# Grouping small matmuls in a planned instruction order, and one vector product for two half tiles

## The chip, the cores and the metric

The kernel runs on one core of one Trainium2 chip, as one program in one launch. The metric is device time in microseconds, from plain runs without the profiler; a further run was made with the hardware profiler, and its rows are quoted. An engine is named as in the profile: PE is TensorE (matmuls; PEld is its weight load), DVE is VectorE, ACT is ScalarE, POOL is GpSimd, SP is the queue that issues DMAs.

## The reference

One layer of a diffusion backbone: 1024 latent tokens and 256 context tokens, width 1024, float32. In order: a modulated SwiGLU feed-forward half step, token mixing, a second feed-forward half step, a final norm. The change lies in token mixing:

```python
def gla_chunked(q, k, v, g, s0):               # 4 heads, dk 64, dv 128, both directions
    b = cumsum(gc, axis=-2)
    rel = exp(where(tri, b_i - b_j, -inf))     # a decay per key feature
    scores = einsum('id,jd,ijd->ij', qc, kc, rel)
    o = scores @ vc + (qc * exp(b)) @ s
    s = exp(b_last) * s + (kc * exp(b_last - b)).T @ vc

def retention_chunked(q, k, v, s0, log_gamma): # 4 heads, dk 128, dv 128, both directions
    scores = (qc @ kc.T) * decay
    o = scores @ vc + (qc * q_dec) @ s
    s = chunk_dec * s + (kc * k_dec).T @ vc
```

Both run forward and backward; latent scans start from the final states of the context scans. The inputs of both are column blocks of one projection `h @ w_in`, and the outputs are normalised, gated with silu of another block and projected with `w_out`.

## The kernel before

**Projections and small products.** A projection multiplies a float32 value split into a high and a low float32r part: three products (high by high, low by high, high by low; `mm3`, lines 401 to 404) of 128x512, 128x288 or 128x256 into a `psa` bank of PSUM. A weight half is loaded to `raw`, ScalarE rounds it to `whi`, VectorE subtracts to `wlo` (`split`, 396 to 398). Everything else on TensorE in mixing works in float32 and writes `psb` banks: transposes against the identity, the products of the scans, and the level products. A float32 matmul shows as two records of TensorE, a transpose as one. There are four `psa` and four `psb` banks.

**The gated scan in levels** (`gla_mix`, 1555 on). For a head and a half of the latent tokens (`tg` 0 and 1) the tile A holds queries of the forward direction on partitions 0 to 63 and keys of the backward one on 64 to 127, B the other two. For half sizes hs of 1, 2, 4, 8, 16, 32, 64, blocks of 2 hs tokens are scored across their middle. Up to hs 16, four copies (two on VectorE, two on ScalarE) bring the halves into zeroed tiles zq and zk, and sixteen matmuls with 32 columns (32 records) make the level's scores in a `psb` bank, which VectorE merges into `cm` or `sc` by a mask. For 32 and 64 the matmuls read A and B directly, in 64x32 and 64x64 pieces. At the end of each level A's upper halves and B's lower halves are multiplied by the decays of the level (lines 1608 to 1611), two VectorE products:

```python
bc = lambda i: e[:, :, i:i + 1].to_broadcast([P, 256 // hs, hs])
nc.vector.tensor_tensor(out=blk(a)[:, :, hi], in0=blk(a)[:, :, hi], in1=bc(0), op=ALU.mult)
nc.vector.tensor_tensor(out=blk(bb)[:, :, lo], in0=blk(bb)[:, :, lo], in1=bc(1), op=ALU.mult)
```

**The gate columns.** `proj_v` (1334) projects the values of two heads, and the first pair's projection carries 32 gate columns: for each of four chunks of 128 tokens the values are copied from `psa` to `vt`, the gate columns to a tile `p89` of two buffers, and that is transposed at once. `ctx_gla` and `ctx_ret` compute the context states of each head; `ctx_ret` scales its values by decays with four `tensor_scalar` products on VectorE before its two 128x256 matmuls.

**What sets the order.** From the second half step's end to the last mixing head, operations aren't issued as they are called: `Recorder` (168 on) keeps them with their reads and writes, and `run` (290 on) makes a list schedule. Each operation has a planned cost (`COST` and `add`, 204 on; VectorE, ScalarE and GpSimd costs times `GROW`, 1.05). `run` repeatedly takes, over all engines, the engine whose next operation can start first, and on it, among those that are ready at that time, the one called earliest. An operation is ready when its predecessors have ended in the plan (plus 0.4 us where TensorE waits for another engine) and its buffers are free. The order found is fixed on each engine, including SP's queue of DMAs; the engines work through their lists in order, and real waits are semaphores. The instructions of this stage all show as line 142 in the profile, so they are told apart by tile. The output projection behind it (`mixed_out`) isn't recorded; its first products come between the last transposes.

Of the kernel before, what the change touches and what calls it, by code (L numbers as in the profile page):

```python
# [11 lines left out]
F32 = mybir.dt.float32  # L12
F32R = mybir.dt.float32r
AF = mybir.ActivationFunctionType
ALU = mybir.AluOpType
PSUM = bass.MemoryType.PSUM

P = 128
# [29 lines left out]
class View:  # L48
# [64 lines left out]
    def bitcast(self, dtype):  # L113
        return self.step(lambda t: t.bitcast(dtype), self.dims)

    def get(self):
        t = self.root.real
        for f in self.how:
            t = f(t)
        return t  # L120
# [40 lines left out]
class Recorder:  # L161
# [42 lines left out]
    def add(self, eng, call, outs, ins, name, a, k):  # L204
        n = lambda v: int(np.prod(v.shape[1:]))
        size = max([n(v) for v in outs] + ([n(v) for v in ins] if name in ("tensor_reduce", "bn_stats") else []) + [1])
        bytes, func = 0, None
        if eng == "PE":
            if name == "transpose":
                cost = 0.11 * size / P  # L210
            elif (a[2].root if isinstance(a[2], View) else a[2]).dtype == F32R:
                cost = (size + 32) / 2400
            else:
                cost = size / 600 + 0.01 if size > 64 else size * 0.0011
        elif eng == "SP":
            v = (outs or ins)[0]
            cost, bytes = 0.42, 4 * size * v.shape[0]
        else:
            base, each = COST.get((eng, name)) or COST[eng]
            cost = 1.2 if k.get("op") == ALU.pow else base + size * each if size > 32 else 0.19  # L220
            if name == "activation":
                func = (a[2] if len(a) > 2 else k["func"])
        op = Op(eng, call, cost, outs, ins, name, bytes, FSET.get(func))
        op.port = eng == "POOL" or name in SHARED and not any(self.psum(v.root) for v in ins)
        (self.ops if self.group is None else self.group).append(op)

# [66 lines left out]
    def run(self):  # L293
        self.link()
        self.rank()
        self.last = {}
        free = {"PE": 0.0, "DVE": LEAD, "ACT": LEAD, "POOL": LEAD, "SP": LEAD}
        port = {"DVE": LEAD, "POOL": LEAD}
        cand, table, pipe, order = [o for o in self.ops if not o.left], None, LEAD, []
        while cand:  # L300
            best = None
            byeng = defaultdict(list)
            for o in cand:
                if o.eng is None:
                    best = (-1e9, o)
                    break
                t = self.room(o)
                if t is not None:
                    for p in o.pre:
                        t = max(t, p.end + (0 if p.eng == o.eng else LATPE if p.eng == "PE" else TOPE if o.eng == "PE" else LATE))  # L310
                    byeng[o.eng].append((t, o.key, o))
            if best is None:
                for eng, os in byeng.items():
                    if eng in port:
                        other = port["DVE" if eng == "POOL" else "POOL"]
                        os = [(max(t, other) if o.port else t, i, o) for t, i, o in os]
                    s = max(free[eng], min(t for t, _, _ in os))
                    o = min((i + (TSW if eng == "ACT" and o.func and o.func != table else 0), i, o) for t, i, o in os if t <= s + 1e-6)[2]
                    if best is None or s < best[0]:
                        best = (s, o)  # L320
            s, o = best
            cand.remove(o)
            if o.eng is None:
                o.end = max((p.end for p in o.pre), default=-1e9)
            else:
                c = o.cost * (1 if o.eng in ("PE", "SP") else GROW)
                if o.eng == "ACT" and o.func and o.func != table:
                    table, c = o.func, c + 1.3
                o.end = s + c
                free[o.eng] = o.end - OVER.get(o.eng, 0)  # L330
                if o.port:
                    port[o.eng] = free[o.eng]
                if o.eng == "SP":
                    pipe = max(pipe, s) + o.bytes / 300e3
                    o.end = max(pipe, s) + DLAT
# [24 lines left out]
        assert len(order) == len(self.ops)  # L360
        t = self.trunk
        t.nc, t.tc = self.nc, self.tc
        del t.tile
        for n, v in self.kept.items():
            setattr(t, n, v)
        return order


class Trunk:
# [964 lines left out]
    def proj_v(self, pr, gla, vt, pool):  # L1334
        nc = self.nc
        for tg in LATTG:
            ps = [self.psA() for _ in range(4)]
            gate = self.v_proj(tg, pr, gla, ps)
            if gate:
                pT = self.psB()  # L1340
            for c in range(4):
                nc.scalar.copy(vt[:, 4 * tg + c, :], ps[c][:, :256])
                if gate:
                    r = self.tile(pool, [P, P], F32, "p89", 2)
                    nc.scalar.copy(r.rearrange("p (k r) -> p k r", k=4), ps[c][:, 256:288].unsqueeze(1).to_broadcast([P, 4, 32]))
                    nc.tensor.transpose(pT[:, c * P:(c + 1) * P], r, self.ident)
            if gate:
                self.p89T[tg] = self.tile(pool, [P, 512], F32R, f"p89T{tg}", 1)
                self.stack(self.p89T[tg], pT, (64, 96))

# [204 lines left out]
    def gla_mix(self, h, vt, qp, kp, sg, gt, pool):  # L1555
        nc = self.nc
        u = h % 2
        f, b = slice(0, 64), slice(64, 128)
        c3 = lambda t: t.rearrange("p (c t) -> p c t", t=P)
        c32 = lambda t: t.rearrange("p (c t) -> p c t", t=32)  # L1560
        A, B, g, L, sc, big, cm = {}, {}, {}, {}, {}, {}, {}
        us = slice(64 * u, 64 * u + 64)
        for tg in LATTG:
            A[tg], B[tg] = self.tile(pool, [P, 512], F32, f"A{tg}"), self.tile(pool, [P, 512], F32, f"B{tg}")
            for t, sl, src in ((A, f, qp), (A, b, kp), (B, f, kp), (B, b, qp)):
                nc.sync.dma_start(t[tg][sl], src[tg][us])
            g[tg], L[tg] = gt[tg]
        for hs in (1, 2, 4, 8, 16, 32, 64):
            blk = lambda t: t.rearrange("p (n t) -> p n t", t=2 * hs)
            lo, hi = slice(0, hs), slice(hs, 2 * hs)  # L1570
            for tg in LATTG:
                a, bb = A[tg], B[tg]
                if hs <= 16:
# [23 lines left out]
                else:  # L1597
                    for o in range(0, 512, 2 * hs):
                        r = o % P
                        l, m, e = slice(o, o + hs), slice(o + hs, o + 2 * hs), o + 2 * hs  # L1600
                        nc.tensor.matmul(big[tg][r:r + hs, m], bb[f, l], a[f, m], start=True, stop=True)
                        nc.tensor.matmul(big[tg][r + hs:r + 2 * hs, l], a[b, m], bb[b, l], start=True, stop=True)
                if hs == 1:
                    e = g[tg]
                else:
                    o = 512 - 1024 // hs
                    e = L[tg][:, o:o + 512 // hs]
                e = e.rearrange("p (n t) -> p n t", t=2)
                bc = lambda i: e[:, :, i:i + 1].to_broadcast([P, 256 // hs, hs])
                nc.vector.tensor_tensor(out=blk(a)[:, :, hi], in0=blk(a)[:, :, hi], in1=bc(0), op=ALU.mult)  # L1610
                nc.vector.tensor_tensor(out=blk(bb)[:, :, lo], in0=blk(bb)[:, :, lo], in1=bc(1), op=ALU.mult)
                if hs == 8:
                    sc[tg] = g[tg]
                    nc.scalar.copy(sc[tg].rearrange("p (c r t) -> p c r t", c=4, r=4),
# [23 lines left out]
        for i in range(7):  # L1638
            for sl, c, d in ((f, i, i + 1), (b, 7 - i, 6 - i)):
                nc.vector.scalar_tensor_tensor(out=S[sl, d, :], in0=S[sl, c, :], scalar=eT(sl, c),  # L1640
                                               in1=U(sl, c), op0=ALU.mult, op1=ALU.add)
        for tg in LATTG:
            po = self.psB()
            with self.pe_order():
                for c in range(4):
                    s = slice(c * P, (c + 1) * P)
# [443 lines left out]


NT2 = 5
AB = 5
AHEAD = 5
NLOW = 150
# [118 lines left out]
```

## Time and profile before

| | us |
|---|---|
| plain runs, median of 3 | 2107.12 (2106.99 to 2107.57) |
| profiled execution | 2112.04 |
| its span, first to last instruction | 2110.2 |
| mean granted TensorE clock | 0.996 |

The page gives each engine's busy time over the span; the stage view gives it between two times, with the clock granted to TensorE (1.00 is full speed). Matmul durations in the rows are longer than the spacing of their starts, since matmuls are pipelined: what one costs is read from the starts. In rows of instructions in order of time the columns are start, duration, engine, line, operation, output and inputs, size and count; a bracket behind it is idle time of the engine before it and what ended it. In rows of groups there stand busy time, mean ns of one, and idle time ahead with its releasers.

### The profile page before, as it was taken

The numbers are of one execution on the slowest core, as the hardware profiler recorded it, in microseconds if no ns is written. First come the engines' busy times: TensorE is split into PE (matmuls) and PEld (weight loads), VectorE is DVE, ScalarE is ACT, GpSimd is POOL, SyncE is SP. The second block draws the span as 40 slices with busy tenths as digits, with TensorE's granted clock in tenths as the row PEclk, the third lists the DMA queues.
The fourth block names the chain that finished last, engine by engine and source line by source line (L and its number), as shares of the span: only waits on it lengthen the run. The fifth ranks groups of instructions, "written<-read, shape, count | busy, mean of one in ns | idle before, by whom it ended". The sixth has DMA issues, their size and how long they took to land. (4 is left out here: it accounts for less than half of the span.)

```text
span 2110.2 us, 34588 instructions
## 1 busy us (share of the span) xinstructions
PE 2082.0 (99%) x12490; PEld 1779.4 (84%) x12490; DVE 1492.1 (71%) x2750; ACT 983.1 (47%) x1824; POOL 205.4 (10%) x195
## 2 busy tenths in 40 slices
PE   8999999999999999999999999999999999999998
PEld 7888888888889999998788978888788888888888
DVE  7889999866776445864777467867776676665676
ACT  4433433435544445665765346444434334344553
POOL 0000000000016664001011001000000000010000
PEclk9999999999999999999999999999999999999999
DMA  9267867559886553663323333352244444477774
GB/s 339 87 212 233 288 216 253 195 163 355 290 290 222 182 181 103 211 189 110 93 67 109 97 84 93 98 174 67 94 161 140 154 168 149 151 233 226 226 231 149
DMA packets 202972, 373.53 MB, mean 177 GB/s; under 512 B 24336, under 2 KB 37296, under 8 KB 202800
## 3 DMA queue, kind: packets, MB, share of 16 engines
q1 hardware_dynamic: 202368, 371.18, 53.5%
q8 instruction: 98, 1.61, 0.3%
q14 instruction: 74, 0.61, 0.1%
q10 hardware_dynamic: 432, 0.13, 0.0%
HBM read 296.74 MB, written 66.09 MB: 172 GB/s over the span
## 5 line engine op out<-in xcount | busy, mean ns | idle before, releaser
L397 ACT ACTIVATE whi<-raw 128x512 fp32r<-128x512 f32 x403 | 253.8, 631 | 529.1 <-issue 155.9
L398 DVE TENSOR_TENSOR wlo<-raw,whi 128x512 fp32r<-128x512 f32 x403 | 277.2, 690 | 185.4 <-ACT whi L397 184.3
L402 PE MATMUL psa<-hh,whi 128*128 128x512 f32 x772 | 302.3, 392 | 0.1
L403 PE MATMUL psa<-hl,whi 128*128 128x512 f32 x772 | 301.6, 391 | 0.0
L404 PE MATMUL psa<-hh,wlo 128*128 128x512 f32 x772 | 301.4, 391 | 0.0
L403 PE MATMUL psb<-hl,whi 128*128 128x512 f32 x632 | 246.6, 390 | 0.8 <-DVE hl L398 0.8
L404 PE MATMUL psb<-hh,wlo 128*128 128x512 f32 x632 | 246.2, 390 | 0.6 <-DVE wlo L398 0.6
L402 PE MATMUL psb<-hh,whi 128*128 128x512 f32 x632 | 246.1, 389 | 0.5 <-ACT whi L397 0.5
L402 PEld LDWEIGHTS psa<-hh,whi 128*128 128x128 f32 x772 | 145.6, 189 | 31.4 <-ACT s L646 0.7
L404 PEld LDWEIGHTS psa<-hh,wlo 128*128 128x128 f32 x772 | 145.3, 188 | 30.1 <-DVE wlo L398 0.2
L403 PEld LDWEIGHTS psa<-hl,whi 128*128 128x128 f32 x772 | 145.4, 188 | 30.0
L398 POOL TENSOR_TENSOR hl<-s,hh 128x512 fp32r<-128x512 f32 x88 | 138.4, 1599 | 138.8 <-DVE hl L398 80.8
L403 PEld LDWEIGHTS psb<-hl,whi 128*128 128x128 f32 x632 | 118.6, 188 | 27.5 <-DVE hl L398 3.0
L404 PEld LDWEIGHTS psb<-hh,wlo 128*128 128x128 f32 x632 | 118.7, 188 | 25.9 <-DVE wlo L398 1.7
L402 PEld LDWEIGHTS psb<-hh,whi 128*128 128x128 f32 x632 | 118.6, 188 | 25.6 <-ACT whi L397 1.0
L142 DVE TENSOR_TENSOR wlo<-raw,whi 128x512 fp32r<-128x512 f32 (+1 forms) x112 | 70.6, 641 | 88.5 <-ACT whi L142 88.3
L142 PE MATMUL psa<-hh,whi 128*128 128x512 f32 x320 | 129.0, 403 | 0.0
L142 PE MATMUL psa<-hl,whi 128*128 128x512 f32 x320 | 128.6, 402 | 0.0
L142 PE MATMUL psa<-hh,wlo 128*128 128x512 f32 x320 | 128.4, 401 | 0.0
L404 PE MATMUL psa<-hh,hl 128*128 128x256 f32 x392 | 111.1, 284 | 0.0
L402 PE MATMUL psa<-hh,hh 128*128 128x256 f32 x392 | 111.1, 283 | 0.0
L403 PE MATMUL psa<-hl,hh 128*128 128x256 f32 x392 | 110.9, 283 | 0.0
(409 smaller groups left out, 4747.5 us busy)
## 6 DMA issues: line engine op xcount, KB each, us to landing
raw<-in_w SPq DMA_DIRECT2D x242, 256.0 KB, 3.3
s<-in_w SPq DMA_DIRECT2D x198, 256.0 KB, 4.0
gd<-s SPq DMA_DIRECT2D x154, 256.0 KB, 2.8
ada<-in_adaT SPq DMA_DIRECT2D x76, 512.0 KB, 4.6
raw<-gd SPq DMA_DIRECT2D x91, 256.0 KB, 3.5
sd<-s SPq DMA_DIRECT2D x44, 256.0 KB, 2.7
raw<-sd SPq DMA_DIRECT2D x44, 256.0 KB, 3.4
hh<-in_w SPq DMA_DIRECT2D x44, 256.0 KB, 4.1
```

The lines of the kernel that those rows point to most:

```text
L142: self.rec.add(self.eng, lambda: f(*map(get, a), **{x: get(v) for x, v in k.items()}), outs, ins, name, a, k)
L397: nc.scalar.activation(hi, src, AF.Copy)
L398: (eng or nc.vector).tensor_tensor(out=lo, in0=src, in1=hi.bitcast(F32), op=ALU.subtract)
L402: mm(ps, wa[0], xa[0], start=start, stop=False, skip_group_check=more)
L403: mm(ps, wa[0], xa[1], start=False, stop=False, skip_group_check=more)
L404: mm(ps, wa[1], xa[0], start=False, stop=stop, skip_group_check=more)
```

## The change

Three things:

- **The planner.** An operation on TensorE has a kind: float32r (projection) or not. The planner books `TURN`, 0.09 us, on an operation whose kind differs from that of the one before it. While TensorE is among small products, it takes further small ones that are ready; otherwise projections that are ready go first, and a small product only enters the choice when it has been ready for `WAIT` (0.5 us for a matmul, 1.0 us for a transpose). Where no projection is ready, small ones go as before. And a `tensor_scalar` that reads no PSUM is booked with 0.18 us and 0.55 ns an element, where it had 0.2 and 1.1.
- **The gate columns.** The four copies of a half go into one tile of tag `t2` (512 columns, five buffers), and the four transposes follow together.
- **A and B.** They become the halves of one tile AB of 1024 columns, and one product per level multiplies A's upper and B's lower halves, through a view `both` that steps from the one to the other.

```diff
+    def both(self, hs):
+        q = self.dims[0]
+        return self.step(lambda t: bass.AP(t.tensor, t.offset + hs, [t.ap[0], [512 - hs, 2], [2 * hs, 256 // hs], [1, hs]]),
+                         [q, (2, 512 - hs, 1), (256 // hs, 2 * hs, 1), (hs, 1, 1)], (self.off[0], self.off[1] + hs))
...
+            kind = name != "transpose" and (a[2].root if isinstance(a[2], View) else a[2]).dtype == F32R
...
+            if name == "tensor_scalar" and not any(self.psum(v.root) for v in ins):
+                base, each = 0.18, 0.00055
...
                     s = max(free[eng], min(t for t, _, _ in os))
+                    if eng == "PE":
+                        same = [x for x in os if x[2].kind == kind and x[0] <= s + 1e-6]
+                        if same and not kind:
+                            os = same
+                        elif same:
+                            os = [x for x in os if x[2].kind or x[0] + WAIT[x[2].name] <= s]
...
                 c = o.cost * (1 if o.eng in ("PE", "SP") else GROW)
+                if o.eng == "PE" and o.kind != kind:
+                    kind, c = o.kind, c + TURN[o.kind]
...
             if gate:
-                pT = self.psB()
+                pT, r = self.psB(), self.t2(pool)
             for c in range(4):
                 nc.scalar.copy(vt[:, 4 * tg + c, :], ps[c][:, :256])
                 if gate:
-                    r = self.tile(pool, [P, P], F32, "p89", 2)
-                    nc.scalar.copy(r.rearrange("p (k r) -> p k r", k=4), ps[c][:, 256:288].unsqueeze(1).to_broadcast([P, 4, 32]))
-                    nc.tensor.transpose(pT[:, c * P:(c + 1) * P], r, self.ident)
+                    nc.scalar.copy(r[:, c * P:(c + 1) * P].rearrange("p (k r) -> p k r", k=4),
+                                   ps[c][:, 256:288].unsqueeze(1).to_broadcast([P, 4, 32]))
             if gate:
+                with self.pe_order():
+                    for c in range(4):
+                        s = slice(c * P, (c + 1) * P)
+                        nc.tensor.transpose(pT[:, s], r[:, s], self.ident)
...
-            A[tg], B[tg] = self.tile(pool, [P, 512], F32, f"A{tg}"), self.tile(pool, [P, 512], F32, f"B{tg}")
+            ab[tg] = self.tile(pool, [P, 1024], F32, f"AB{tg}")
+            A[tg], B[tg] = ab[tg][:, :512], ab[tg][:, 512:]
...
-                nc.vector.tensor_tensor(out=blk(a)[:, :, hi], in0=blk(a)[:, :, hi], in1=bc(0), op=ALU.mult)
-                nc.vector.tensor_tensor(out=blk(bb)[:, :, lo], in0=blk(bb)[:, :, lo], in1=bc(1), op=ALU.mult)
+                e = e.rearrange("p (n t) -> p t n", t=2).unsqueeze(3).to_broadcast([P, 2, 256 // hs, hs])
+                nc.vector.tensor_tensor(out=ab[tg].both(hs), in0=ab[tg].both(hs), in1=e, op=ALU.mult)
...
+WAIT, TURN = {'transpose': 1.0, 'matmul': 0.5}, (0.09, 0.09)
```

More of the change, by code (lines that the diff above doesn't have):

```diff
@@ L207, in add @@
         bytes, func = 0, None
+        kind = None
         if eng == "PE":
+            kind = name != "transpose" and (a[2].root if isinstance(a[2], View) else a[2]).dtype == F32R
             if name == "transpose":
                 cost = 0.11 * size / P
-            elif (a[2].root if isinstance(a[2], View) else a[2]).dtype == F32R:
+            elif kind:
                 cost = (size + 32) / 2400
@@ L223, in add @@
         op = Op(eng, call, cost, outs, ins, name, bytes, FSET.get(func))
+        op.kind = kind
         op.port = eng == "POOL" or name in SHARED and not any(self.psum(v.root) for v in ins)
@@ L298, in run @@
         port = {"DVE": LEAD, "POOL": LEAD}
+        kind = True
         cand, table, pipe, order = [o for o in self.ops if not o.left], None, LEAD, []
@@ L1560, in gla_mix @@
         c32 = lambda t: t.rearrange("p (c t) -> p c t", t=32)
-        A, B, g, L, sc, big, cm = {}, {}, {}, {}, {}, {}, {}
+        ab, A, B, g, L, sc, big, cm = {}, {}, {}, {}, {}, {}, {}, {}
         us = slice(64 * u, 64 * u + 64)
         for tg in LATTG:
-            A[tg], B[tg] = self.tile(pool, [P, 512], F32, f"A{tg}"), self.tile(pool, [P, 512], F32, f"B{tg}")
+            ab[tg] = self.tile(pool, [P, 1024], F32, f"AB{tg}")
+            A[tg], B[tg] = ab[tg][:, :512], ab[tg][:, 512:]
             for t, sl, src in ((A, f, qp), (A, b, kp), (B, f, kp), (B, b, qp)):
@@ L1607, in gla_mix @@
                     e = L[tg][:, o:o + 512 // hs]
-                e = e.rearrange("p (n t) -> p n t", t=2)
-                bc = lambda i: e[:, :, i:i + 1].to_broadcast([P, 256 // hs, hs])
-                nc.vector.tensor_tensor(out=blk(a)[:, :, hi], in0=blk(a)[:, :, hi], in1=bc(0), op=ALU.mult)
-                nc.vector.tensor_tensor(out=blk(bb)[:, :, lo], in0=blk(bb)[:, :, lo], in1=bc(1), op=ALU.mult)
+                e = e.rearrange("p (n t) -> p t n", t=2).unsqueeze(3).to_broadcast([P, 2, 256 // hs, hs])
+                nc.vector.tensor_tensor(out=ab[tg].both(hs), in0=ab[tg].both(hs), in1=e, op=ALU.mult)
                 if hs == 8:
```

## The prediction

> **What bounds the kernel now.** I read the page's first part, then the busy times by stage on both sides of the mixing, then who TensorE waited for there, then TensorE's instructions in order of time around single small matmuls.
>
> ```profile
> span 2110.2 us, 34588 instructions
> ...
> PE 2082.0 (99%) x12490; PEld 1779.4 (84%) x12490; DVE 1492.1 (71%) x2750; ACT 983.1 (47%) x1824; POOL 205.4 (10%) x195
> ```
>
> ```profile
> core 0: us, PE busy (x) PEld busy (x) DVE busy (x) ACT busy (x) POOL busy (x), PEclk, DMA share, GB/s
> 873.35:928.85 55.50, 55.50 (x451) 55.38 (x449) 39.74 (x76) 35.28 (x81) 6.24 (x11) 1.00 0.67 202
> 928.85:931.00 2.15, 0.29 (x3) 0.06 (x1) 1.83 (x6) 1.36 (x5) 0.00 (x0) 1.00 0.84 236
> 931.00:935.40 4.40, 4.39 (x22) 4.37 (x23) 0.66 (x3) 2.43 (x9) 0.00 (x0) 0.61 0.89 287
> ...
> 975.70:978.30 2.60, 0.68 (x6) 0.48 (x4) 2.56 (x7) 1.83 (x5) 2.28 (x5) 1.00 0.01 3
> ...
> sum 495.95, PE 489.38 PEld 428.76 DVE 330.64 ACT 277.90 POOL 49.59; mean PE 37.64 PEld 32.98 DVE 25.43 ACT 21.38 POOL 3.81
> ```
>
> The recorded stage, whose order the change rewrites, runs from 873.35 to 1369.3 us. TensorE is busy for 489.4 of its 496.0 us, VectorE for 330.6, ScalarE for 277.9. So TensorE is the bound, and a change of order can win only what TensorE loses between and inside its instructions. The view of who waited for whom names all the idle time in that stage:
>
> ```profile
> engine line waited for: us in total, times, longest us
> PE psb L142 <- DVE t L142: 1.9, 1, 1.9
> PE psa L142 <- ACT p L142: 1.9, 1, 1.9
> PE psb L142 <- ACT t L142: 0.9, 3, 0.5
> PE psb L142 <- DVE S L142: 0.6, 1, 0.6
> PE psb L142 <- DVE cm L142: 0.5, 1, 0.5
> PE psb L142 <- ACT zk L142: 0.4, 1, 0.4
> PE psb L142 <- issue: 0.4, 1, 0.4
> ```
>
> That is 6.6 us, of which 4.7 stand before small products (psb) and 1.9 before a projection (psa). Behind the projection's wait (928.85 to 931.00) the granted clock is 0.61 for 4.4 us, which costs another 4.4 x 0.39 = 1.7 us. The second long gap (975.7) has clock 1.00 after it.
>
> **Part 1: fewer turns between projections and small products.** The new planner books 0.09 us whenever TensorE goes from float32r to float32 or back, and holds a small product back until it has been ready for 0.5 us (matmul) or 1.0 us (transpose), unless TensorE is among small ones already. In the two programs' instruction order the runs of float32 work in this stage fall from 155 to 103, and those of one instruction alone from 47 to 4; the 1290 small instructions and the projections stay. What does a turn cost? Lone transposes between projections:
>
> ```profile
> 1296.98 0.40 PE L142 MATMUL psa<-hl,whi 128*128 128x512 f32 x1
> 1297.22 0.27 PE L142 MATMUL psb<-ident,t 128*128 128x128 f32 x1
> 1297.25 0.48 PE L142 MATMUL psa<-hh,wlo 128*128 128x512 f32 x1
> 1297.57 0.27 PE L142 MATMUL psb<-ident,t 128*128 128x128 f32 x1
> ...
> 1298.28 0.48 PE L142 MATMUL psa<-hh,wlo 128*128 128x512 f32 x1
> 1298.59 0.40 PE L142 MATMUL psa<-hh,whi 128*128 128x512 f32 x1
> ```
>
> and a run of eight of the same size:
>
> ```profile
> 1085.77 0.39 PE L142 MATMUL psa<-hh,wlo 128*128 128x512 f32 x1
> 1086.00 0.40 PE L142 MATMUL psa<-hh,whi 128*128 128x512 f32 x1
> 1086.23 1.05 PE L142 MATMUL psb<-qk,qk 128*128 128x128 f32 x8
> 1087.04 0.47 PE L142 MATMUL psa<-hl,whi 128*128 128x512 f32 x1
> 1087.36 0.40 PE L142 MATMUL psa<-hh,wlo 128*128 128x512 f32 x1
> ```
>
> Durations overlap, so I go by starts. A projection product takes 0.23 us from start to start (1085.77 to 1086.00). From 1296.98 to 1298.59 lie 1.61 us: five projection products (5 x 0.228 = 1.14) and four lone transposes, 0.47/4 = 0.118 each. From 1086.00 to 1087.36 lie 1.36 us: two projection products (0.456) and eight records, 0.904/8 = 0.113 each. A transpose alone costs 0.005 more than a record in a run; I take 0.01 for a whole round trip. 52 round trips fewer give **-0.5 us**, not the 52 x 0.18 = 9.4 us that the planner books.
>
> The exception is the matmuls of a level, 32 columns wide:
>
> ```profile
> 1304.07 0.40 PE L142 MATMUL psa<-hl,whi 128*128 128x512 f32 x1
> 1304.39 0.46 PE L142 MATMUL psb<-zq,zk 128*32 128x32 f32 x32
> 1304.78 0.50 PE L142 MATMUL psa<-hh,wlo 128*128 128x512 f32 x1
> 1305.12 0.39 PE L142 MATMUL psa<-hh,whi 128*128 128x512 f32 x1
> ```
>
> ```profile
> 1226.10 0.39 PE L142 MATMUL psa<-hh,wlo 128*128 128x512 f32 x1
> 1226.41 1.35 PE L142 MATMUL psb<-zq,zk 128*32 128x32 f32 x128
> 1227.69 0.50 PE L142 MATMUL psa<-hh,whi 128*128 128x512 f32 x1
> 1228.03 0.40 PE L142 MATMUL psa<-hl,whi 128*128 128x512 f32 x1
> ```
>
> 32 records cost 1.05 - 0.456 = 0.59 us, 128 cost 1.93 - 0.456 = 1.47: 0.0092 per further record and 0.30 fixed per block. Here merging pays, but the change merges by data type, not by tile shape. Counted in the order, there are 47 blocks of such narrow matmuls before and 47 after: several levels do come together, but transposes and 128-wide products now get in between them (one narrow matmul, two transposes, fifteen narrow ones). So **0**; one block more or less is 0.3 us. [...]
>
> **Part 2: the margins.** A small product that starts a run now comes 0.5 or 1.0 us after it is planned ready. The held-back work waits in the written order, not on the engine: what runs instead are projections, and the copies behind the small product on ScalarE and VectorE start up to 1 us later. Against plan errors this is slack. The waits of 0.9, 0.6, 0.5, 0.4 and 0.4 us (2.8 together, each single one 0.6 or less) are of the size that the margins cover, but the margin is only for the first of a run; those that join it have none. Bounds are 0 and -2.8; I take half, **-1.4**. The wait of 1.9 us (975.7) is for the value scaling of a context head. In the new order the corresponding scaling stands before, no longer behind, the 64x512 product of A, which is 0.7 us in the row below, and has 0.5 us of margin: **-1.2**. The wait for `p` (1.9 us plus 1.7 of clock) stays: ScalarE's order there (two conversions of late weight tiles, then the copies that free the psa banks) is the same in both programs, and the transposes that moved are not what it waits for: **0**.
>
> **Part 3: one product for A and B.**
>
> ```profile
> L142 DVE TENSOR_TENSOR A<-A,L 128x256 f32<-128x256 f32 x48 | 20.1, 418 | 3.8 <-PE psb L142 1.8 <-ACT zk L142 1.7
> L142 DVE TENSOR_TENSOR B<-B,L 128x256 f32<-128x256 f32 x48 | 20.0, 417 | 0.8 <-ACT zq L142 0.6
> ...
> L142 DVE TENSOR_TENSOR qk<-qk,rs 128x512 f32<-128x512 f32 x16 | 11.0, 687 | 0.2
> ...
> L142 DVE TENSOR_TENSOR A<-A,sc 64x512 f32<-64x512 f32 x8 | 5.4, 677 | 0.7 <-ACT zq L142 0.6
> ```
>
> Two products of 0.418 become one of 512 elements, 0.687 by the nearest row: 0.15 us less for each of 7 levels x 2 halves x 4 heads = 56, or 8.3 us of VectorE. It hides wholly behind TensorE (VectorE idles a third of this stage), so **0** on the path. Against it: the joint product waits for all four copies of its level, of which ScalarE makes two (0.4 us each); before, A's product could run while ScalarE still copied from B. That may cost back some 0.1 us a level, on VectorE's chain and again not on the bound.
>
> **Part 4: the rest.** Eight lone transposes of the gate columns become two groups of four; their source moves from tag p89 to t2 (five buffers), and the copies stay: 0, in the turns above. The planner's price for a tensor_scalar from SBUF falls to the measured length (512 elements: 0.46 instead of 0.76); that moves order alone. New waits in an order that no trace shows: from 0 to the present 4.7 us; I take **+0.6**, a lower figure than today's since most runs now start with a margin.
>
> **Sum.** -0.5 + 0 - 1.4 - 1.2 + 0 + 0.6 = -2.5 us. Outside this stage nothing moves: the first product of the output projection stands within 3 us of work of its old place, with the last transposes interleaved alike. The profiled execution took 2112.04 us, its span 2110.2 with 1.8 around it; the sum is made there and would give 2109.5. The three plain runs have a median of 2107.12, 4.9 less, and the sum applied to it gives **2104.6 us**.
>
> **Rivals.**
> - *Nearly all waits before small products go* (4.7), with 0.5 for turns and 0.9 of waits too short to show as idle time (my estimate: a product is drawn 0.39 us long at a spacing of 0.23, so up to 0.16 of each hides): -6.1, 2101.0 us. For it: every wait but one is shorter than the margin of a transpose. Against it: the members that join a run have none. 0.22.
> - *The turn is real*, and the planner's 0.18 a round trip is saved: -9.4 - 2.0 = 2095.7. The rows of lone transposes speak against it. 0.06.
> - *Slower: the plan makes TensorE late, and the chip has it early.* The planner books 103 x 0.18 = 18.5 us of turns, and the rows show 1.0. So TensorE comes 17.5 us (3.5% of 496) sooner than planned, while the other engines are planned only 5% longer than their costs. Where the lead of VectorE or ScalarE at a joined product is below 0.17 us for each run since they last waited, TensorE waits in the middle of a run. A third of 17.5 is +5.8, or 2112.5 with the turns. Against it: VectorE is idle for 165 of the 496 us and so catches up often; the margins are several times 0.17. It decides once leads are under about 0.5 us. 0.14. A new gap of 2 us can also cost clock: 1.7 us, as behind 928.85. [...]
> - *The joint product stretches the level chain* and a few small products wait for it: +2, 2109. 0.08.
>
> **How the numbers follow.** The forecast has 0.50, with a range of its own from 2101.5 to 2108. A measurement of this kernel can tell about 0.2%, 4.2 us, from no change: faster is below 2102.9, slower above 2111.3. Faster: most of the first rival (0.18), the second (0.06) and a tail of the forecast (0.06): 0.30. Slower: 0.13 of the third and 0.01 elsewhere: 0.14. The rest is 0.56. The range from 2098.5 to 2111.0 leaves out the second rival (0.06) and most of the third (0.12).
>
> **What would show it.** In the new profile the stage's summed TensorE idle time should be 3 to 5 us instead of 6.6, with the wait for the psa copies (now from t2) and the clock dip still there; lone or first transposes should still add 0.11 to 0.12 us between projections; a narrow block 0.59; the joint product 0.69 at every level. Wrong would be: a stage shorter by 9 us with the same idle time (the turn is real), or several waits of psb inside runs that sum to over 8 us (the overbooked turns).

## The result and the profile after

| | before | after |
|---|---|---|
| median of 22 executions each, us | 2108.34 (2105.22 to 2111.43) | 2111.47 (2107.46 to 2116.31) |
| ratio | | 1.0016, 95% interval 1.0009 to 1.0023 |
| profiled execution, its span, us | 2112.04, 2110.2 | 2108.48, 2106.7 |
| recorded stage, us | 873.35 to 1369.27 = 495.92 | 870.59 to 1368.08 = 497.49 |
| granted clock, mean of the executions | 0.9953 to 0.9959 in four series | 0.9954 |

The change costs 3.3 us (1.9 to 4.8) where 2.5 us less was forecast. The profiled execution of after is one of its fastest and shorter than that of before, but not because of this stage: it comes to the stage 2.8 us earlier and needs 2.3 us less behind it, where the same work stands but for four products of 0.23 us. Over all the versions below, the start of the stage lies anywhere from 870.1 to 875.1 us and the rest behind it takes 735.4 to 740.9. So only the stage is compared, and it is longer.

The page of after, first part:

```profile
span 2106.7 us, 34491 instructions
...
PE 2080.5 (99%) x12490; PEld 1780.4 (85%) x12490; DVE 1491.0 (71%) x2694; ACT 980.0 (47%) x1822; POOL 205.3 (10%) x195
```

56 VectorE instructions are gone, as many as there were levels, and TensorE has its 12490 as before. Its stage by windows (length, then busy time and count of each engine, then the granted clock):

```profile
926.09:927.90 1.81, 0.29 (x4) 0.07 (x2) 1.78 (x6) 1.29 (x5) 0.00 (x0) 1.00 0.93 261
927.90:932.00 4.10, 4.10 (x32) 4.09 (x33) 1.76 (x5) 2.92 (x10) 0.00 (x0) 1.00 0.85 252
...
971.80:975.00 3.20, 1.49 (x9) 1.09 (x8) 2.80 (x7) 2.81 (x7) 2.82 (x6) 1.00 0.12 41
...
1109.50:1110.60 1.10, 0.42 (x2) 0.00 (x0) 1.10 (x5) 0.94 (x3) 0.00 (x0) 1.00 0.01 4
...
sum 497.51, PE 490.39 PEld 430.57 DVE 329.36 ACT 275.55 POOL 49.38; mean PE 54.49 PEld 47.84 DVE 36.60 ACT 30.62 POOL 5.49
```

The wait before the psa copies (926.09) and that of the context head (971.80) are both still there, a new one has come at 1109.50, and the half-speed stretch behind the first (0.61 before) is missing in this execution. The idle time by who was waited for:

```profile
PE psb L147 <- ACT t L147: 3.1, 4, 1.7
PE psa L147 <- ACT t L147: 1.5, 1, 1.5
PE psa L147 <- issue: 0.9, 1, 0.9
PE psb L147 <- DVE S L147: 0.5, 1, 0.5
PE psb L147 <- ACT zq L147: 0.4, 1, 0.4
PE psb L147 <- ACT zk L147: 0.3, 1, 0.3
PE psb L147 <- issue: 0.2, 1, 0.2
```

That sums to 6.9 us, against 6.6 before and the 3 to 5 that the prediction named. But this view understates: a record is drawn longer than the spacing of the starts (a projection product of 512 columns 0.39 us or more, at 0.2275), so the start of a wait is hidden under the record before it. I therefore measure waits from start to start: each distance between two records of the stage, less the undisturbed spacing of its kind, read from the starts in the two traces (0.2275 for a projection product of 512 columns, 0.12 for one of 256, 0.111 for a 128-wide record, 0.0093 for a narrow one, 0.3 more for each narrow block), and less what a half-speed stretch costs. In this measure before waits **10.25 us** and after **13.0 us**. The remainder is 483.97 us before (495.92 - 10.25 - 1.7 of clock) and 483.56 after (497.49 - 13.0 - 0.9 for four products of the output projection that now lie inside the stage). The stage is 2.35 us longer, of the 3.3 measured. Since the measure takes a record's share as fixed, the remainder can't show a dearer or cheaper record, and whatever goes beyond the share counts as wait.

One thing in it is no wait: inside a block of narrow products, a change between 128x32 and 64x32 or 64x64 tiles. Two neighbouring blocks of 64 narrow records in after, the first of one tile shape, the second of two:

```profile
1021.64 0.76 PE L147 MATMUL psb<-zq,zk 128*32 128x32 f32 x64
1022.33 0.50 PE L147 MATMUL psa<-hh,whi 128*128 128x512 f32 x1
1022.85 0.46 PE L147 MATMUL psb<-zq,zk 128*32 128x32 f32 x32
1023.24 0.45 PE L147 MATMUL psb<-AB 64*32 64x32 f32 x32
1023.62 0.50 PE L147 MATMUL psb<-p89T,wg 128*128 128x512 f32 x1
```

From the block's first record to the next projection lie 0.69 us (1021.64 to 1022.33) and 0.77 us (1022.85 to 1023.62), so the change cost 0.08 here. The stage has 5 such changes before and 14 after: by this pair 0.7 us of the 2.75 are that (an estimate, 9 x 0.08), and some 2 us are waits.

Where the waits stand, taking those over 0.3 us up to 20 us ahead of the stage's end, each put to the record that it stands before: ahead of the first of a run of small products 3.9 us before and 1.9 after; ahead of a product that joined a run 2.0 and **3.9**; ahead of projections 2.0 and 2.8. One of the joined ones, in the timeline of after (start, duration, engine):

```profile
1028.55 1.29 ACT L147 ACTIVATE t<-t 128x512 f32<-128x512 f32 x2
...
1028.87 0.40 PE L147 MATMUL psa<-hl,whi 128*128 128x512 f32 x1
1029.19 0.32 PE L147 MATMUL psb<-zq,zk 128*32 128x32 f32 x12
...
1029.75 0.35 ACT L147 COPY t<-psb 128x256 f32<-128x256 f32 x1
...
1030.16 0.71 PE L147 MATMUL psb<-t,t 128*128 128x128 f32 x4 [0.65 <-ACT t L147]
```

A run begins at 1029.19 with narrow products of a level. Twelve records in, the list has two products of `t`. Their copy on ScalarE starts at 1029.75, behind two activations that began at 1028.55, and TensorE stands in the middle of its run. 52 narrow records of the same level are queued behind it.

The planner's arithmetic, written out for after, shows how little such products had to spare. Of seven waits over 0.3 us ahead of joined products, five stand where the plan has the product ready 0.01 to 0.14 us before its turn comes (beyond the 0.4 us of latency that it always allows), the other two where it has 0.6 and 1.3.

### The profile page after: what moved, and what is told of

It is laid out like the page before. It is cut to its first block, busy times and chain, and to the rows that moved or that the text cites. A ratio compares the mean times of both kernels' runs of the same rounds, so it can differ in the third digit from the quotient of the medians.

```text
span 2106.7 us, 34491 instructions
## 1 busy us (share of the span) xinstructions
PE 2080.5 (99%) x12490; PEld 1780.4 (85%) x12490; DVE 1491.0 (71%) x2694; ACT 980.0 (47%) x1822; POOL 205.3 (10%) x195
## 4 chain that ended last, share of the span: by engine, by line
PE 91%; DVE 3%; ACT 3%; DMA 2%; issue 1%; SPq 0%; POOL 0%; DVEq 0%; POOLq 0%; ACTq 0%
PE psa L147 14%; PE psa L421 14%; PE psa L423 13%; PE psa L422 13%; PE psb L423 10%; PE psb L422 10%; PE psb L421 10%; PE psb L147 5%; DMA raw<-in_w 1%; ACT t L147 1%; ACT L147 1%; DVE hl L579 0%; DVE junk L483 0%; PE psb L559 0%; DVE nt L573 0%
```

## The experiments

All are measured against before, in executions on the same chip. "Waits" is the start-to-start measure above, changes of tile shape included, in the one profiled execution of each version; the difference in us is the ratio times 2108.

| version | turn booked, us | ratio (95% interval) | us | waits, us | waits against before |
|---|---|---|---|---|---|
| after | 0.09 | 1.0016 (1.0009 to 1.0023) | +3.3 | 13.0 | +2.75 |
| e1_planner | 0.09 | 1.0062 (1.0050 to 1.0075) | +13.1 | 19.4 | +9.1 |
| e2_ab | none | 1.0005 (0.9995 to 1.0014) | +1.0 | 9.85 | -0.4 |
| e3_p89 | none | 0.9997 (0.9989 to 1.0006) | -0.6 | 9.6 | -0.7 |
| e4_noturn | 0 | 0.9998 (0.9990 to 1.0007) | -0.4 | 10.4 | +0.1 |
| e6_turn18 | 0.18 | 1.0057 (1.0045 to 1.0069) | +12.0 | 21.7 | +11.5 |
| e7_turn02 | 0.02 | 0.9983 (0.9975 to 0.9992) | -3.6 | 8.6 | -1.65 |
| e10_planner0 | 0 | 0.9998 (0.9989 to 1.0006) | -0.4 | 10.8 | +0.55 |
| e9_join | 0 | 0.9987 (0.9978 to 0.9995) | -2.7 | 9.3 | -0.95 |
| e11_grow9 | 0.09 | 1.0015 (1.0006 to 1.0024) | +3.2 | 12.3 | +2.05 |
| e12_grow1 | 0 | 1.0013 (1.0004 to 1.0022) | +2.7 | 12.9 | +2.65 |
| e13_join02 | 0.02 | 0.9992 (0.9982 to 1.0001) | -1.7 | 7.9 | -2.3 |
| e14_nomargin | 0 | 0.9988 (0.9978 to 0.9997) | -2.5 | 8.9 | -1.35 |
| e15_tope6 | 0.09 | 0.9997 (0.9989 to 1.0006) | -0.6 | 10.35 | +0.1 |
| e16_join09 | 0.09 | 1.0004 (0.9996 to 1.0013) | +0.8 | 11.2 | +0.95 |

The last two columns with numbers in us agree within 2 us in every row but e1's, whose rest is clock (below): across fifteen orders the time goes with what the records take beyond their share, and not with the number of runs of small products, which goes from 102 (e6) to 150 (e3). The waits ahead of joined products, in the count above, are 3.9 us in after, 4.9 in e11, 4.5 in e12 and 8.1 in e6, which are all slower, and 2.3 or less in e2, e3, e7, e9, e10 and e13 to e16, which aren't. The exception is e4: 4.3 us, of which 2.2 are one wait, and no loss of time.

### Which part costs: e1 to e4

Theory W: the new order's waits cost. M: the joint product of A and B stretches the chain of a level. C: longer float32 runs bring half-speed stretches.

e1_planner is before with the planner's part alone:

```diff
+            if name == "tensor_scalar" and not any(self.psum(v.root) for v in ins):
+                base, each = 0.18, 0.00055
...
+                    if eng == "PE":
+                        same = [x for x in os if x[2].kind == kind and x[0] <= s + 1e-6]
+                        if same and not kind:
+                            os = same
+                        elif same:
+                            os = [x for x in os if x[2].kind or x[0] + WAIT[x[2].name] <= s]
...
+                if o.eng == "PE" and o.kind != kind:
+                    kind, c = o.kind, c + TURN[o.kind]
...
+WAIT, TURN = {'transpose': 1.0, 'matmul': 0.5}, (0.09, 0.09)
```

> Only the planner's part of the change (kinds, WAIT, TURN, the cheaper tensor_scalar); gate columns and A, B as before. Theory W (the new order's waits, not the merged work, cost the time): 2 to 4 us slower than before, stage idle time of TensorE 7 to 8 us. Theory M (the joint product stretches the level chain and the planner part is harmless): within 1 us of before. Theory C (longer float32 runs make the clock drop more often): slower by 2 to 4 us, and the runs' mean clocks lower than those of before by 0.001 on the average, with idle time as before.

Measured +13.1 us: more than the whole change, and far above what any of the three theories allowed. Its timeline, where one run of small products takes 17 us:

```profile
1137.01 1.16 PE L142 MATMUL psb<-vt,t 128*128 128x128 f32 x8 [0.31 <-ACT t L142]
...
1138.36 3.79 DVE L142 SCALAR_TENSOR_TENSOR S<-S,L,psb 64x128 f32<-64x128 f32 x10
...
1141.14 0.76 PE L142 MATMUL psb<-vt,sc 128*128 128x128 f32 x2 [2.97 <-DVE S L142]
...
1145.60 0.60 ACT L142 ACTIVATE t<-psb 128x512 f32<-128x512 f32 x1 [8.00 <-PE psb L142]
...
1150.21 0.48 PE L142 MATMUL psb<-ident,t 128*128 128x128 f32 x1 [4.64 <-ACT t L142]
```

TensorE waits 2.97 us for VectorE's ten steps of `S`, then goes on with pairs of `S` products, and ScalarE waits 8.00 us for a psb result that comes out of this run. Only then can ScalarE start (1145.60) the chain of a normalisation, which ends with the `t` that the next transpose of the list reads, and TensorE waits 4.64 us for it. The clock at that place:

```profile
1139.60:1153.30 13.70, 7.21 (x31) 6.65 (x32) 4.56 (x11) 5.78 (x11) 3.11 (x8) 0.50 0.05 18
```

13.7 us at 0.50, with 7.21 us of TensorE work in it. Two 128-wide records came every 0.43 us there (1142.80 to 1143.23), against 0.22 at clock 1.00 in after (1079.23 to 1079.45), so about half of the 7.21 is clock: an estimated 3.6 us beside the 9.1 of waits. The executions' mean clock is 0.9933, against 0.9958 of before's in the same series. These two waits are not TensorE ahead of its plan: the planner's arithmetic, written out, has idle times of 3.7 and 5.5 us at these two places already. Here the booked turn led the planner to an order that is worse by its own account.

e2_ab (before with the joint product alone):

```diff
-                nc.vector.tensor_tensor(out=blk(a)[:, :, hi], in0=blk(a)[:, :, hi], in1=bc(0), op=ALU.mult)
-                nc.vector.tensor_tensor(out=blk(bb)[:, :, lo], in0=blk(bb)[:, :, lo], in1=bc(1), op=ALU.mult)
+                nc.vector.tensor_tensor(out=ab[tg].both(hs), in0=ab[tg].both(hs), in1=e, op=ALU.mult)
```

> Only the joint product for A and B; planner and gate columns as before. Theory M: 2 to 4 us slower, with TensorE waits behind cm, zk or S above the 1.5 us of before. Theory W: within 1.5 us of before either way, since VectorE's 8 us lie beside TensorE. Joint product 0.69 us at every level for both.

e3_p89 (before with the four gate transposes grouped, their source from tag t2):

```diff
-                    r = self.tile(pool, [P, P], F32, "p89", 2)
...
+                pT, r = self.psB(), self.t2(pool)
...
+                with self.pe_order():
+                    for c in range(4):
```

> Only the gate columns' grouping (one t2 tile, four transposes together). Both theories: within 1 us of before; the wait for the psa copies (1.9 us) stays. If the t2 buffer is short, the context heads start later and a wait of 1 us appears there.

Neither can be told from no change (+1.0 and -0.6, both intervals hold 1). M finds no support: e2 is below its 2 to 4 us, and its waits are not above those of before. Together with the planner's part, though, the two turn +13.1 into +3.3: they do nothing measurable by themselves, but the planner meets another list and falls another way.

e4_noturn is the whole change with the turn not booked:

```diff
-WAIT, TURN = {'transpose': 1.0, 'matmul': 0.5}, (0.09, 0.09)
+WAIT, TURN = {'transpose': 1.0, 'matmul': 0.5}, (0.0, 0.0)
```

> The change with TURN 0, so that a turn is booked at what the rows of before show (0.01 us or less). Theory W in the form that overbooked turns make the plan late: recovers 2 to 3 us of the 3.1, idle time of the stage back to 5 to 6 us. If the loss comes from another part, it stays within 1 us of the change.

-0.4: the whole loss goes with one constant, while grouping stays (105 runs, 9 of one instruction; after has 103 and 4). But where the time came back is not where it was lost: in its profile waits ahead of joined products are still 4.3 us, and those ahead of first ones and of projections 1.3 each (after 1.9 and 2.8). C is not what costs after: after's executions have a mean clock of 0.9954, 0.0005 at most below a series of before, which is 1 us of 2108, and its profile has no half-speed stretch in the stage. In e1 it is some 4 of 13 us.

### Is it the booking, or any new order? e6, e7, e10, e9

e6, e7 and e10 change the constant alone: the whole change with TURN at 0.18 and at 0.02, and the planner's part alone (e1) with 0. Theories S (the booking) and X (chance) are told in the expectations.

```diff
-WAIT, TURN = {'transpose': 1.0, 'matmul': 0.5}, (0.09, 0.09)
+WAIT, TURN = {'transpose': 1.0, 'matmul': 0.5}, (0.18, 0.18)
```

> The whole change, with the booked turn doubled to 0.18 us each way: 102 runs x 0.36 = 36.7 us that the plan books and TensorE does not need. Theory S (the booked turns are the cause: TensorE comes earlier than planned and waits inside its runs): the waits grow with the booking, so at least the 3 us of the whole change and likely twice as much, +5 to +10 us against before. Theory X (any other order of this length draws its waits by chance, whatever the turn is booked at): anywhere between -1 and +12 us, with no trend from 0 over 0.09 to 0.18. Below +2 us, S falls.

> The whole change, with the booked turn lowered to 0.02 us each way: 103 runs x 0.04 = 4.1 us booked in vain. Theory S: a lead of 4 us over 496 is covered by the 5% that the other engines are planned longer, so within 1.5 us of before, like the version with no turn booked (-0.1). Theory X: a new draw, as likely +3 or +12 as 0. Above +3 us, S falls.

> The planner's part alone, as in the run that took +12.5 us, but with no turn booked. Its order has 108 runs, 8 of them of one instruction. Theory S: the long wait inside a run goes with the 19 us of booked turns, and the time comes back to within 2 us of before. Theory X: a new draw; +5 us or more is as likely as 0. The trace says in either case which product waits and whether it joined a run or began one.

+12.0, -3.6, -0.4. Only e10 is inside S's range; e6 lies above it and e7 below. But the direction is that of S: 0.02, 0.09 and 0.18 give -3.6, +3.3 and +12.0, and e1's order goes from +13.1 to -0.4, where X had no trend. The two waits of e1 are gone in e10. e6's waits by who was waited for, the first row:

```profile
PE psb L147 <- ACT t L147: 8.5, 7, 2.1
```

Waits of small products for a copy of `t` on ScalarE, the kind shown for after, are 8.5 us in seven places where after has 3.1 in four. The run that after begins at 1029.19 looks like this in e6:

```profile
1025.77 0.40 PE L147 MATMUL psa<-hl,whi 128*128 128x512 f32 x1
1026.10 0.45 PE L147 MATMUL psb<-zq,zk 128*32 128x32 f32 x28
1027.86 0.71 PE L147 MATMUL psb<-t,t 128*128 128x128 f32 x4 [1.31 <-ACT t L147]
```

1.31 us idle where after has 0.65. Waits before the first of a run have grown too, to 6.3 us, three of them over 1.5 us although each product had the margin of 0.5 us. And e7's waits, all rows:

```profile
PE psb L147 <- ACT t L147: 1.9, 3, 1.3
PE psa L147 <- ACT t L147: 1.2, 1, 1.2
PE psb L147 <- DVE AB L147: 0.6, 1, 0.6
PE psb L147 <- DVE t L147: 0.5, 1, 0.5
PE psb L147 <- issue: 0.2, 1, 0.2
```

4.4 us together, where before has 6.6.

e9_join keeps the turn at 0 and gives the members of a run a margin:

```diff
-                        if same and not kind:
-                            os = same
-                        elif same:
+                        proj = any(x[2].kind and x[0] <= s + 1e-6 for x in os)
+                        late = [x for x in same if x[0] + JOIN <= s + 1e-6 or not proj]
+                        if late and not kind:
+                            os = late
+                        elif proj:
...
+JOIN = 0.4
```

> The whole change with no turn booked, and a margin for the members of a run as well: while a projection is ready, a small product joins a run only if it has been ready for 0.4 us by the plan. 120 runs, 22 of one instruction. Theory S with its corollary (the waits that are left stand before members of a run, which have no margin): waits before small products fall from 9 to some 6 us, -1 to -3 us against before. Theory X: a new draw around 0, and the waits before members of a run stay as large as those before the first of a run.

-2.7, as S had it. In the same count as above, waits ahead of members fall to 0.8 us (e4 4.3), and those ahead of the first of a run are 2.3.

### How the booking costs: e11, e12, e15, e16

If TensorE's lateness against the other engines, summed over the stage, is what counts, then planning the others longer cancels it. GROW is the factor on the durations of VectorE, ScalarE and GpSimd.

e11 takes 1.09 for it with the turn at 0.09, e12 takes 1.01 with the turn at 0.

```diff
-LEAD, LATE, LATPE, TOPE, TSW, MIX, GROW, DLAT = -6.0, 0.1, 0.2, 0.4, 0, 1, 1.05, 3.5
+LEAD, LATE, LATPE, TOPE, TSW, MIX, GROW, DLAT = -6.0, 0.1, 0.2, 0.4, 0, 1, 1.09, 3.5
```

> The whole change with its turn booked at 0.09 us, but the work of VectorE, ScalarE and GpSimd planned 9% longer than its costs instead of 5%: 4% of a stage of 496 us, 20 us, about what the turns book in vain. Theory S (what counts is that TensorE is planned too slow against the other engines): the two errors cancel, the 3.1 us come back, and the time is between -3 and +1 us of before. Rival R (booking a turn spoils the choices themselves, whatever the other engines are planned at): still +3 us or more.

> The whole change with no turn booked (-0.1 us as it was measured), and the work of the other engines planned only 1% longer than its costs instead of 5%: they come later against TensorE by up to 20 us over the stage, as if 19 us of turns were booked. Theory S: the waits come back without any turn, +3 to +12 us against before. Rival R: no turn is booked, so within 1.5 us of before.

e11 took +3.2: nothing came back, as R had it, and theory S in this form falls. e12 took +2.7, just under S's range and above R's, with an interval (+0.8 to +4.6) that reaches into both: it decides little, though time taken from the other engines' plan seems to cost as well, with no turn booked. So the sum over the stage is hardly the right quantity. Theory L puts the loss in each run: a run begins, the plan gives its members 0.18 us per round trip that the chip doesn't take, and a member that is planned ready by less than that isn't. Against it stands R: the booking leads to worse orders by itself.

e15 changes TOPE, the latency that the plan allows from another engine's result to TensorE; e16 is e9's edit with the turn at 0.09.

```diff
-LEAD, LATE, LATPE, TOPE, TSW, MIX, GROW, DLAT = -6.0, 0.1, 0.2, 0.4, 0, 1, 1.05, 3.5
+LEAD, LATE, LATPE, TOPE, TSW, MIX, GROW, DLAT = -6.0, 0.1, 0.2, 0.6, 0, 1, 1.05, 3.5
```

> The whole change, turn booked at 0.09 us, and the latency that the plan allows from any other engine's result to a TensorE instruction raised from 0.4 to 0.6 us: every small product is planned 0.2 us later behind its producer, about what one booked round trip (0.18 us) gives away. Theory L (the booking costs locally: each run that is booked too long lets its later members be planned ready when on the chip they are not): the waits of joined products fall from 4.1 us back to some 2, and the time comes to within 1.5 us of before, or below it. Rival R (booking turns leads the plan to other choices that are worse by themselves, whatever the leads): +3 us or more again.

> The whole change, turn booked at 0.09 us, and a margin of 0.4 us for the members of a run while a projection is ready (with no turn booked, that margin stands at -2.8 us). Theory L: 0.4 us cover two booked round trips, so the waits of joined products go and the time is between -3 and +1 us of before. Rival R: +3 us or more.

e15 took -0.6, with 107 runs and every turn booked as in after: what L forecast, and against R (+3 or more). The same run as above, in e15:

```profile
1030.97 0.40 PE L147 MATMUL psa<-hh,whi 128*128 128x512 f32 x1
1031.30 0.25 PE L147 MATMUL psb<-zq,zk 128*32 128x32 f32 x2
1031.58 0.71 PE L147 MATMUL psb<-t,t 128*128 128x128 f32 x4
1032.22 0.75 PE L147 MATMUL psb<-zq,zk 128*32 128x32 f32 x62
```

The same 64 narrow records and four of `t` pass without a wait. The waits of joined products, counted as above, are 1.8 us (after 3.9); the expectation had 2. e16 took +0.8, inside L's range but at its edge: waits before members fall to 0.8 us, and new waits of 1.6 ahead of the first of a run (1050.44) and 1.3 ahead of a projection (985.51) take part of the gain back. Both are one order each, and orders differ by 2 to 3 us with edits that should do nothing, so L rests on the two together with the leads in the plan of after. For e1, whose plan had the long waits in it, R is the account.

### What the margin is worth, and the best version: e14, e13

e13 is e9's edit with the turn at 0.02, e14 is e4 with this:

```diff
-WAIT, TURN = {'transpose': 1.0, 'matmul': 0.5}, (0.0, 0.0)
+WAIT, TURN = {'transpose': 0.0, 'matmul': 0.0}, (0.0, 0.0)
```

> The whole change with no turn booked and no margin before the first of a run (0 instead of 0.5 and 1.0 us); runs are still not left for a projection while a small product is planned ready: 131 of them, 27 of one instruction. Part 2 of the prediction (margins shrink the waits, by 1.4 us and more): +1.4 to +4 us against the version with margins and no turn booked, which stands at -0.1. Rival (a margin for the first alone is worth nothing, since the members that join wait): within 1 us of it.

> The margin of 0.4 us for the members of a run (-3.1 us with no turn booked) and the turn at 0.02 us (-3.2 us without that margin) together. If each takes away waits of its own: -5 to -6 us. If both only keep the leads of the other engines long enough, they overlap: -2 to -4 us. If their gains were chance draws: around 0.

e14 took -2.5, outside both of its expectations: the time is not shorter with the margin before the first of a run. Without it the stage waits 8.9 us, with it (e4) 10.4. In the count above the margin does what it is for, 3.1 us of waits ahead of first ones without it and 1.3 with it, but ahead of members there stand 1.6 and 4.3: the wait has moved. e13 took -1.7: the two gains do not add. The best that was run is the whole change with the turn at 0.02 us, 0.17% (0.08 to 0.25) faster than before and 6.4 us under the median of after. Beside orders that differ by 2 to 3 us with edits that should do nothing, I would not read 0.02 as better than 0; that both are better than 0.09 is what the runs show.

## Why the prediction was wrong

- **What bounds the kernel**: right. TensorE is busy for 490.4 of 497.5 us, and what moves the time is what it loses between and inside its instructions.
- **Part 1, the turn**: right, as far as the runs can tell. The rival that the turn is real (-11.4) falls, and a run of 24 records between projections in after (1079.00 to 1082.14, less two projections) comes to 0.112 each, where a lone transpose of before was 0.118. No run isolates the forecast of -0.5. The 0 for tile shapes was too low: the 47 blocks did stay 47, but nine more changes of shape came inside them, +0.7 us by the pair of rows above. A narrow block itself costs what it did:

```profile
1104.86 0.40 PE L147 MATMUL psa<-hh,whi 128*128 128x512 f32 x1
1105.19 0.46 PE L147 MATMUL psb<-zq,zk 128*32 128x32 f32 x32
1105.58 0.50 PE L147 MATMUL psa<-hl,whi 128*128 128x512 f32 x1
1106.01 0.46 PE L147 MATMUL psb<-zq,zk 128*32 128x32 f32 x32
1106.40 0.50 PE L147 MATMUL psa<-hh,wlo 128*128 128x512 f32 x1
1106.73 0.39 PE L147 MATMUL psa<-hh,whi 128*128 128x512 f32 x1
```

From 1104.86 to 1106.73 lie 1.87 us, less three projections of 0.228: 1.19 for two blocks, 0.59 each.

- **Part 2, the margins**: failed in two ways. The small waits before the first of a run did go (3.9 to 1.9 us in all, so -2.0 for a forecast of -2.6 on all waits before small products), but the large one stayed. Its place in after:

```profile
970.87 1.30 ACT L147 ACTIVATE t<-t 128x512 f32<-128x512 f32 x2
...
972.59 0.35 ACT L147 COPY t<-psb 128x256 f32<-128x256 f32 x1
972.81 0.28 DVE L147 TENSOR_SCALAR t<-t,kdf 128x128 f32<-128x128 f32 x1
972.84 0.63 ACT L147 ACTIVATE whi<-raw 128x512 fp32r<-128x512 f32 x1
...
973.38 0.36 ACT L147 COPY t<-psb 128x256 f32<-128x256 f32 x1
973.59 0.27 DVE L147 TENSOR_SCALAR t<-t,kdf 128x128 f32<-128x128 f32 x1
...
973.81 0.68 PE L147 MATMUL psb<-t,t 128*128 128x256 f32 x2 [1.71 <-ACT t L147]
```

The scaling did move ahead of the product of A, and starts 0.2 us behind its copy. But the copies themselves wait on ScalarE, behind activations and a conversion of `whi`: I had read the last waiter, VectorE, and not what stood behind it on ScalarE. The second reason of this part, that a margin shortens the time that is waited in all, is not borne out by e14: there it moved to the members.

- **Part 3, the joint product**: right. Its row, against an estimate of 0.687:

```profile
L147 DVE TENSOR_TENSOR AB<-AB,L 128x512 f32<-128x512 f32 x48 | 32.2, 685 | 8.2 <-ACT zk L147 4.6 <-PE psb L147 3.0
```

- **Part 4, the new waits**: this is the step that failed, and with it the sign. I took +0.6, "since most runs now start with a margin". The members that join a run have none, and their waits alone went from 2.0 to 3.9 us, +1.9; a new wait of 1.1 before the projection of 1110.86, for which the profile names no releaser, took those before projections from 2.0 to 2.8. That is +2.7 for the +0.6. The sign named for the overbooked turns, waits inside runs of over 8 us, didn't come: it was 3.9. I had both halves in hand: the planner's 9.4 us too much in Part 1, and the members without margin in Part 2. In the sum I counted the overbooking as a gain that doesn't come, and not as a cost.
- **The rival that was slower** had the mechanism, and got 0.14. Its size (a third of 17.5, +5.8) came from the sum of the booked turns over the stage, which e11 speaks against; what counts, by e15 and the leads in the plan, is the lead that each run's members keep. That it decides "once leads are under about 0.5 us" fits: 0.2 us more lead (e15) was enough, 0.4 us for members alone (e16) nearly.
- Not settled: why planning the other engines 4% longer (e11) gives nothing back. On a copy of 0.35 to 0.7 us that is 0.01 to 0.03 us, far less than 0.18 for a run, which would explain it; this was only argued. Nor why e4 loses no time with 4.3 us of waits ahead of members in its profile. Nor is it settled how much of one version's figure is the fall of its order: the joint product and the gate columns moved the planner's cost from 13.1 to 3.3 us.

## What to carry to other kernels

A planner's constant that books time the chip doesn't take is not a harmless reserve: it can make the bounding engine arrive before its operands, and the wait stands in the middle of a group, in front of other work. Measure the constant first (here 0.01 us per round trip against 0.18 booked), and try slack as latency on every edge into the bounding engine (e15) rather than as time on the engine itself. A margin for the first of a group alone moves the wait to the members. Before crediting a new order with fewer waits, follow the wait's releaser back to the engine on which its own input stood in line.

## What the runs showed of the hardware

In the profiles of before, e1 and e4 half-speed stretches were about one, two or four times 3.4 us long. The 4.4 us at 0.61 in before are 3.41 at 0.50 (931.99 to 935.40), and ahead of its stage stand 6.83 us (20.63 to 27.46) and 3.41 us (30.87 to 34.28) at 0.50; e1 had 13.7 us at 0.50, and e4 this, 3.4 us at 0.50, behind a wait inside a run of transposes:

```profile
1340.80:1344.90 4.10, 2.06 (x15) 1.45 (x14) 1.51 (x4) 1.97 (x6) 2.10 (x1) 1.00 0.00 0
1344.90:1348.30 3.40, 3.40 (x13) 2.92 (x13) 3.40 (x6) 3.35 (x7) 0.00 (x0) 0.50 0.25 87
```

Those in the stage of before and in e4 followed gaps of about 2 us, 2.15 (928.85 to 931.00) and 2.31 (1341.04 to 1343.35) from start to start; that of e1 began 1.4 us into the idle time of 2.97 us that ends at 1141.14. But not every such gap was followed by one: behind that of 1.98 us in after (971.83 to 973.81) and that of 2.20 us in before (975.72 to 977.92) the clock stayed at 1.00. So the length of the gap doesn't tell them apart, since 2.15 us cost clock and 2.20 us did not; what does, these runs don't show.
